# Mixing stage: query head sums in column groups, low-rank products in row halves, v centred by head in its transpose, and no place pads

## The chip, the cores and the metric

The kernel runs on one core of a Trainium2 chip. A core has five engines with a queue each: PE (TensorE; the loading of its weights is listed apart, as PEld), DVE (VectorE), ACT (ScalarE), POOL (GpSimd) and SP (SyncE, which here only issues transfers). Each engine takes its instructions in the order of its queue; engines wait for each other by semaphores. [...] The metric is device microseconds for one execution, the median of the runs shown.

## The reference

Two layers of a decoder trunk on 512 tokens of width 1024, in float32. A layer is a half-step SwiGLU feed-forward, a mixing sub-layer, and another half-step feed-forward, each behind a modulated RMS norm. The change lies in the mixing sub-layer, which has three head groups side by side: attention with a window of 128 and sinks (8 query heads, 2 key heads of 64), RWKV-7 time mixing (4 heads of 64) and a short convolution. What matters of it:

```python
# attention: q and k are normed by head
q = rms_norm(q.reshape(B, T, ATT_Q_HEADS, HEAD_DIM), q_gain)
...
# RWKV: decay and rate come from low-rank products
w_log = -jax.nn.softplus(-(w0 + jnp.tanh(wd) @ w_w2).astype(f32)) - 0.5
a = jax.nn.sigmoid((a0 + ad @ w_a2).astype(f32))
...
def step(S, inp):
    r_t, w_t, k_t, v_t, kk_t, a_t = inp
    s_kk = jnp.einsum('bhvk,bhk->bhv', S, kk_t)
    S = (S * w_t[:, :, None, :] - s_kk[..., None] * (kk_t * a_t)[:, :, None, :]
         + v_t[..., None] * k_t[:, :, None, :])
    return S, jnp.einsum('bhvk,bhk->bhv', S, r_t)
...
mean = jnp.mean(y, axis=-1, keepdims=True)
var = jnp.mean(jnp.square(y - mean), axis=-1, keepdims=True)
y = ((y - mean) * lax.rsqrt(var + RWKV_GN_EPS)).reshape(B, T, RWKV_WIDTH) * gn_w + gn_b
bonus = jnp.sum(r * k * r_k, axis=-1, keepdims=True) * v
```

The recurrence is linear in v, and each row of the state belongs to one element of v. So if v has mean zero over a head, y has too.

## The kernel before

Activations are held transposed: 128 channels on the partitions, 512 tokens along them. Large products are split in two float32r parts of each operand and made of three matmuls (`mm3`, L117 to L123): `ps_mm` products of 512 columns, or of 256 in the feed-forward, where a block scheme with sums of operands (`com`) saves products. Small products of the mixing stage are plain float32: PE makes two passes for one such matmul, and the trace records each pass (a transpose is one).

The mixing sub-layer (`mix`, L583) is written as generators. `products` (L634) makes the input projection in twenty tiles of 128 channels in the order k, v, four tiles of q, then those of RWKV and the convolution, and later the first part of the output projection. `rwkv(q)` (L745) runs for two head pairs, `attention` (L985) for four blocks of 128 tokens. A loop (L1081 to L1094) steps the live generators and, by the figures that these yield and by RWKV_WORK, ATT_WORK and FILL_WORK (L35), deals out product steps between them. The order of each engine's queue then comes from the framework's scheduler, which goes by priorities and its own estimate of times: instructions of one product step can get between those of another generator, and an ordering edge between two instructions, or a block of high priority, changes that.

Where the change touches it:

- **Query head sums** (L670 to L688). Each q tile holds two heads of 64 channels. It is copied to `qr`, squared by ACT (`qsq`), and for each block of 128 tokens the square is the weight (128x128) and `bones2` (two columns, one for each head) the moving operand: `ps_q` gets tokens on the partitions and two sums. ACT takes the root into `rq`, DVE the reciprocal after the fourth tile. `attention` uses `rq` as a scale by token in its softmax (L1015 to L1026); its score tiles (`ps_sc`) and the sums take their PSUM banks from the same two ("x").
- **Low-rank products** (L752 to L756). `lo` holds tanh(wd) in partitions 0 to 63 and ad in 64 to 127, `lw` the two matrices likewise. `ps_w` and `ps_a` are one matmul each, of 64 rows, 128 columns of weights and 512 of moving operand.
- **v turned** (`tmajor`, L850; `tcopy(v_[q], "vN")`, L868). The recurrence needs v with tokens on the partitions: four transposes into `ps_vN`, a copy by ACT.
- **Mean over a head** (L964 to L966). `headsum` (L608) multiplies y by `bones`, the block matrix of ones of a head, into `ps_m`; DVE subtracts the mean. Then follow the square (`gnsq`), its head sum (`ps_v`), the root (`gnrs`), the reciprocal and the scaling, the gate (`ps_g`), and the split of y for the last output products (`yrH`, `yrL`, L1097 to L1110).
- **Places.** `con` holds the constants (L52; the first 128 columns are loaded at the start, L145, the rest at L1214). A pad of GAP = 448 bytes a partition stands ahead of the pools of `hn` (L67), one of 64 behind them (L70), and two of the same sizes around `com` in the feed-forward (L345, L347). So `hn` and `com` lie 448 bytes, modulo 512, off the weights `wH` and `wL`, and `act` and all that is behind lies level with them.

Of the kernel before, what the change touches and what calls it, by code (L numbers as in the profile page):

```python
# [8 lines left out]
F32 = mybir.dt.float32  # L9
F32R = mybir.dt.float32r  # L10
I32 = mybir.dt.int32
AF = mybir.ActivationFunctionType
ALU = mybir.AluOpType
AXL = mybir.AxisListType
ORDER = mybir.DependencyInfo(mybir.DependencyClass.NoSync, mybir.DependencyReason.DATA)
SYNC = mybir.DependencyInfo(mybir.DependencyClass.Sync, mybir.DependencyReason.DATA)

P = 128
D = 1024
T = 512  # L20
# [6 lines left out]
NB = T // P  # L27
CH = 64
# [3 lines left out]
PAD = 24  # L32
GAP = 448
GROUPS = ((0, 12), (12, 22))
RWKV_WORK, ATT_WORK, FILL_WORK = 29.8, 15.2, 129.6  # L35


def _columns(spec):
# [13 lines left out]
CON, NCON = _columns((  # L52
    ("ident", P), ("bones", P), ("bones2", 2), ("su", CH), ("iu", CH), ("diag", CH),
    ("lev0", CH), ("lev1", CH), ("i64", CH), ("mc", P), ("mp", P), ("mq", P),
# [4 lines left out]
def trunk_kernel(ctx, tc, ins, out, layers=L, phases=("ffn1", "mix", "ffn2")):  # L59
    nc = tc.nc  # L60
# [5 lines left out]

    shift = ctx.enter_context(tc.tile_pool(name="shift", bufs=1))  # L67
    shift.tile([P, GAP // 4], F32, name="shift")
    hnp = [ctx.enter_context(tc.tile_pool(name=n, bufs=KD)) for n in ("hnp", "hnp2")]
    shift = ctx.enter_context(tc.tile_pool(name="shift2", bufs=1))  # L70
    shift.tile([P, (512 - GAP) // 4], F32, name="shift2")
    sp = ctx.enter_context(tc.tile_pool(name="sp", bufs=2))
    ps = ctx.enter_context(tc.tile_pool(name="ps", bufs=4, space=PSUM))
    dram = ctx.enter_context(tc.tile_pool(name="dram", bufs=1, space=bass.MemoryType.DRAM))
    tt, stt, ts = nc.vector.tensor_tensor, nc.vector.scalar_tensor_tensor, nc.vector.tensor_scalar
    act, mm = nc.scalar.activation, nc.tensor.matmul
# [7 lines left out]
    def psum(shape, name, tag="x"):  # L84
        return ps.tile(shape, F32, name=name, tag=tag, bufs=2)
# [87 lines left out]
    def cst(name):  # L173
        a, b = CON[name]
        return con[:, a:b]
# [161 lines left out]
    def ffn(l, w_in, w_pair, w_out, hn, im, ss, need, then, first, ready, coming):  # L337
# [6 lines left out]
        with tc.tile_pool(name="act", bufs=1) as ap_:  # L344
            ap_.tile([P, GAP // 4], F32, name="gap", tag="gap")  # L345
            com = {n: tuple(ap_.tile([P, 4, H2], F32R, name=x, tag="com", bufs=8) for x in ("comH", "comL")) for n in ("P1", "P2", "T3", "T4")}
            ap_.tile([P, (512 - GAP) // 4], F32, name="gap2", tag="gap2")  # L347
            n_first = 2 if first is None else 4
# [234 lines left out]
    def mix(l, hn, ss, mp, then, ready):  # L583
# [18 lines left out]
        def EA(name):  # L602
            return mp.tile([P, T], F32, name=name, tag="ea", bufs=3)
# [4 lines left out]
        def headsum(src, name, tag="x"):  # L608
            pt = psum([P, T], name, tag)
            mm(pt, cst("bones"), src, start=True, stop=True)  # L610
            return pt

        chunks = lambda t: t.rearrange("p (c t) -> p c t", t=CH)
        blocks = lambda t: t.rearrange("p (b c) -> p b c", c=P)
# [19 lines left out]
        def products():  # L634
# [33 lines left out]
            rq = small("rq", NB * 8)  # L668
            rq4 = rq.rearrange("p (b i g) -> p b i g", i=4, g=2)
            for i in range(4):  # L670
                pt = yield from tile_()
                copied = nc.scalar.copy(pt.like(qr[:, i]), pt.view)
                if i == 0:
                    latest["act"] = copied
                if i == 1:
                    pk = headsum(ksq, "ps_ks")
                    rk = EA("rk")
                    act(rk, pk, AF.Sqrt, bias=vals["eps"], scale=1.0 / CH)
                    nc.vector.reciprocal(rk, rk)
                    stt(kt, kt, gqk, rk, ALU.mult, ALU.mult)  # L680
                sq = EA("qsq")
                act(pt.like(sq), pt.view, AF.Square)
                yield
                pq = psum([P, NB, 2], "ps_q")
                for b in range(NB):
                    mm(pq[:, b], sq[:, b * P : (b + 1) * P], cst("bones2"), start=True, stop=True)
                act(rq4[:, :, i], pq, AF.Sqrt, bias=vals["eps64"])
            nc.vector.reciprocal(rq, rq)  # L688
            got.update(kt=kt, V=V, qr=qr, rq=rq)
            done.add("att")  # L690

            got["lo"] = shifted((yield from tile_()), 6, S(1, "lo"))
            act(got["lo"][:64], got["lo"][:64], AF.Tanh)
            for q in range(2):
# [50 lines left out]
        def rwkv(q):  # L745
# [6 lines left out]
            pw = psum([P, T], "ps_w", R)  # L752
            mm(pw, lw[:64, cw], lo[:64], start=True, stop=True)
            pa = psum([P, T], "ps_a", R)
            mm(pa, lw[64:, cw], lo[64:], start=True, stop=True)
            yield 1.7  # L756
            kp = prm(l, "kk")[:, c1]
# [92 lines left out]
            def tmajor(src, name):  # L850
                pt = psum([P, NB, P], name, R)
                for b in range(NB):
                    nc.tensor.transpose(pt[:, b], src[:, b * P : (b + 1) * P], cst("ident"))
                return pt
# [108 lines left out]

            pm = headsum(y, "ps_m", R)  # L964
            stt(y, pm, -1.0 / CH, y, ALU.mult, ALU.add)
            yield 0.9  # L966
            sq = EQ(q, "gnsq")
# [322 lines left out]
def lay_out(i):  # L1290
# [58 lines left out]

    con = [r == s, r // CH == s // CH, r // CH == np.arange(2)[None, :], u < v, u <= v]  # L1350
    con += [u // BASE == v // BASE, lower(4, u, v), lower(5, u, v)]
# [19 lines left out]
```

## Time and profile before

| | |
|---|---|
| median of 3 runs | 1866.85 us (1865.7 to 1868.2) |
| the profiled execution | 1866.04 us |
| its span, first to last instruction | 1864.0 us |
| mean granted PE clock | 0.994 |
| mixing sub-layer, layer 0 | about 390 to 615 us |
| mixing sub-layer, layer 1 | about 1304 to 1529 us |

A row of the timeline gives the start, the duration, engine, line and operation, the tile written and those read, and the number of instructions merged in the row; in brackets the idle time ahead of it and what ended it. Matmuls are pipelined, so one that is listed with 0.38 us takes PE for less: the steps between starts tell the price. A row of the grouped view gives busy time and mean nanoseconds of one instruction. A row of waits gives microseconds in total, times, and the longest.

### The profile page before, as it was taken

To read this page: it belongs to the slowest core of one execution; us is meant where nothing else is said; L and a number is where in the kernel's file an instruction comes from. 1 tells how busy PE (TensorE), PEld (TensorE's weight loads), DVE (VectorE), ACT (ScalarE), POOL (GpSimd) and SP (SyncE) were. 2 spreads that over 40 slices of the span, in tenths; PEclk is the share of its full clock that TensorE was granted. 3 is DMA by queue.
4 is the path that set the end of the run, shared out by engine and by line. 5 is a ranking of instruction groups with operands and counts; after the bars stand their busy time and mean duration, and the time that the engine had idled before them with its cause. 6 is when DMAs were issued, how large, how long until landed. Compare 5 with 4: busy or idle time off the path is not lost.

```text
span 1864.0 us, 33421 instructions
## 1 busy us (share of the span) xinstructions
PE 1828.7 (98%) x13664; PEld 1644.4 (88%) x13664; DVE 1398.4 (75%) x2202; ACT 836.3 (45%) x1272; POOL 130.9 (7%) x212
## 2 busy tenths in 40 slices
PE   8999999999999999999999999999999999999999
PEld 6889899986777999899999988999767788998998
DVE  7687677867986887777878786777589778874872
ACT  4443255346422555245345524544563335532551
POOL 0101110100000000110100020110000000100100
PEclk8999999999999999999999999999999999999999
DMA  7667876621122475886737688773212125775752
GB/s 307 225 185 234 263 197 202 221 83 46 58 55 72 136 195 176 296 223 195 246 112 197 171 272 228 192 229 114 101 56 59 53 68 161 209 227 139 203 144 68
DMA packets 104313, 308.24 MB, mean 165 GB/s; under 512 B 23392, under 2 KB 24416, under 8 KB 103136
## 3 DMA queue, kind: packets, MB, share of 16 engines
q1 hardware_dynamic: 75936, 203.34, 32.3%
q0 software_dynamic: 28224, 102.77, 21.7%
q8 instruction: 107, 1.75, 0.4%
q14 instruction: 46, 0.38, 0.1%
HBM read 302.66 MB, written 3.41 MB: 164 GB/s over the span
## 4 chain that ended last, share of the span: by engine, by line
PE 71%; DVE 13%; DMA 7%; issue 4%; ACT 4%; POOL 1%; SPq 0%; POOLq 0%; DVEq 0%; ACTq 0%
PE ps_mm L121 11%; PE ps_mm L122 10%; PE ps_mm L123 10%; PE ps_d L420 6%; PE ps_d L422 6%; PE ps_d L421 6%; PE ps_f L420 3%; PE ps_f L422 3%; PE ps_f L421 3%; DMA wada<-in_wadaT 2%; DVE wL L135 2%; PE ps_g L422 2%; PE ps_g L420 2%; PE ps_g L421 2%; ACT wH L133 1%
## 5 line engine op out<-in xcount | busy, mean ns | idle before, releaser
L133 ACT CAST wH<-wraw 128x1024 fp32r<-128x1024 f32 (+2 forms) x292 | 266.1, 918 | 434.7 <-PE ps_mm L122 190.2
L135 DVE TENSOR_TENSOR wL<-wraw,wH 128x1024 fp32r<-128x1024 f32 (+2 forms) x292 | 307.2, 1058 | 105.1 <-ACT wH L133 104.4
L123 PE MATMUL ps_mm<-actH,wL 128*128 128x512 f32 (+1 forms) x784 | 281.5, 359 | 2.8 <-DVE wL L135 2.8
L121 PE MATMUL ps_mm<-actH,wH 128*128 128x512 f32 (+1 forms) x784 | 281.6, 359 | 0.0
L122 PE MATMUL ps_mm<-actL,wH 128*128 128x512 f32 (+1 forms) x784 | 281.2, 359 | 0.0
L121 PE MATMUL ps_mm<-hnH,wH 128*128 128x512 f32 (+1 forms) x760 | 267.5, 359 | 5.7 <-ACT hnH L133 2.9
L122 PE MATMUL ps_mm<-hnL,wH 128*128 128x512 f32 (+1 forms) x760 | 266.5, 353 | 0.5
L123 PE MATMUL ps_mm<-hnH,wL 128*128 128x512 f32 (+1 forms) x760 | 266.4, 353 | 0.6 <-DVE wL L135 0.6
L420 PE MATMUL ps_d<-comH,wH 128*128 128x256 f32 x816 | 224.7, 275 | 0.3 <-ACT s L446 0.3
L421 PE MATMUL ps_d<-comL,wH 128*128 128x256 f32 x816 | 224.4, 275 | 0.0
L422 PE MATMUL ps_d<-comH,wL 128*128 128x256 f32 x816 | 224.4, 275 | 0.0
L192 DVE SCALAR_TENSOR_TENSOR wada<-wada,crep 128x1024 f32<-128x1024 f32 x140 | 167.7, 1219 | 48.8 <-DMA wada<-in_wadaT 48.2
L135 DVE TENSOR_TENSOR wL<-sum,wH 128x1024 fp32r<-128x1024 f32 x102 | 124.9, 1224 | 71.5 <-ACT wH L133 71.3
L123 PEld LDWEIGHTS ps_mm<-actH,wL 128*128 128x128 f32 x784 | 149.1, 190 | 20.3 <-DVE wL L135 3.6
L121 PEld LDWEIGHTS ps_mm<-hnH,wH 128*128 128x128 f32 x760 | 143.4, 191 | 24.9 <-issue 3.8
L121 PEld LDWEIGHTS ps_mm<-actH,wH 128*128 128x128 f32 x784 | 149.1, 190 | 16.8
L122 PEld LDWEIGHTS ps_mm<-actL,wH 128*128 128x128 f32 x784 | 149.0, 190 | 16.8
L123 PEld LDWEIGHTS ps_mm<-hnH,wL 128*128 128x128 f32 x760 | 145.5, 191 | 19.3 <-issue 4.3
L122 PEld LDWEIGHTS ps_mm<-hnL,wH 128*128 128x128 f32 x760 | 145.4, 192 | 17.2 <-DVE hnL L277 1.6
L420 PEld LDWEIGHTS ps_d<-comH,wH 128*128 128x128 f32 x816 | 156.7, 192 | 0.9 <-ACT s L446 0.9
L422 PEld LDWEIGHTS ps_d<-comH,wL 128*128 128x128 f32 x816 | 156.7, 192 | 0.0
L421 PEld LDWEIGHTS ps_d<-comL,wH 128*128 128x128 f32 x816 | 156.7, 192 | 0.0
(354 smaller groups left out, 3855.6 us busy)
## 6 DMA issues: line engine op xcount, KB each, us to landing
wada<-in_wadaT POOLq DMA_DIRECT2D x128, 512.0 KB, 4.8
wraw<-in_wmi SPq DMA_DIRECT2D x40, 512.0 KB
wraw<-in_w2p SPq DMA_DIRECT2D x36, 512.0 KB
wraw<-in_w1p SPq DMA_DIRECT2D x32, 512.0 KB
wraw<-in_w1o SPq DMA_DIRECT2D x32, 384.0 KB
wraw<-in_w2o SPq DMA_DIRECT2D x32, 384.0 KB
wraw<-in_w1i SPq DMA_DIRECT2D x20, 512.0 KB
wraw<-in_w1o SPq DMA_DIRECT2D x32, 320.0 KB
```

The lines of the kernel that those rows point to most:

```text
L121: mm(acc, wH, xH, start=start, stop=False)
L122: mm(acc, wH, xL, start=False, stop=False)
L123: mm(acc, wL, xH, start=False, stop=stop)
L133: nc.scalar.copy(hi, src)
L135: return nc.vector.tensor_sub(lo, src, hi.bitcast(F32))
L192: stt(w, w, 1.0, crep, ALU.mult, ALU.mult, accum_out=out_)
L420: mm(acc, wH, xH, start=start and i + k == 0, stop=False, skip_group_check=True)
L421: mm(acc, wH, xL, start=False, stop=False, skip_group_check=True)
L422: mm(acc, wL, xH, start=False, stop=k == 3, skip_group_check=True)
```

## The change

Query head sums: the squares of all four q tiles are kept. When the fourth is there, four matmuls take `bones2`, now 32 columns of which two are not zero, as the weight and one square each as the moving operand, and write partitions 0 to 31, 32 to 63, 64 to 95 and 96 to 127 of one PSUM tile; they are put behind each other by ordering edges (`after`) at high priority. One root over the whole tile goes into the place of the first square, four transposes bring tokens to the partitions, and the reciprocal reads them from PSUM.

Low-rank products: each is cut in two halves of 256 columns, and the four matmuls alternate between rows 0 to 63 and 64 to 127, chained the same way; the two head pairs are in one chain. The yield behind them is 1.2 in place of 1.7.

v is turned by a matmul with `cen`, the identity less 1/64 within a head, in place of the transposes, so it comes out centred. The mean of y and its subtraction go, with their yield of 0.9. RWKV_WORK falls from 29.8 to 28.9.

All four place pads go. `con` grows by 158 columns.

```diff
-GAP = 448
-RWKV_WORK, ATT_WORK, FILL_WORK = 29.8, 15.2, 129.6
+RWKV_WORK, ATT_WORK, FILL_WORK = 28.9, 15.2, 129.6
...
-    ("ident", P), ("bones", P), ("bones2", 2), ("su", CH), ("iu", CH), ("diag", CH),
+    ("ident", P), ("bones", P), ("bones2", 32), ("cen", P), ("su", CH), ("iu", CH), ("diag", CH),
...
-    shift = ctx.enter_context(tc.tile_pool(name="shift", bufs=1))
-    shift.tile([P, GAP // 4], F32, name="shift")
     hnp = [ctx.enter_context(tc.tile_pool(name=n, bufs=KD)) for n in ("hnp", "hnp2")]
-    shift = ctx.enter_context(tc.tile_pool(name="shift2", bufs=1))
-    shift.tile([P, (512 - GAP) // 4], F32, name="shift2")
...
-            ap_.tile([P, GAP // 4], F32, name="gap", tag="gap")
             com = {n: tuple(ap_.tile([P, 4, H2], F32R, name=x, tag="com", bufs=8) for x in ("comH", "comL")) for n in ("P1", "P2", "T3", "T4")}
-            ap_.tile([P, (512 - GAP) // 4], F32, name="gap2", tag="gap2")
...
+        def after(m, other):
+            tc.add_manual_dep(m.ins, other.ins.name, ORDER, reason="parts of the array run together")
+            return m
...
+            sqs = []
             for i in range(4):
...
-                sq = EA("qsq")
-                act(pt.like(sq), pt.view, AF.Square)
+                if i % 2 == 0:
+                    sqs += (lambda t: [t[:, 0], t[:, 1]])(U(1, "qsq", [P, 2, T]))
+                behind = act(pt.like(sqs[i]), pt.view, AF.Square)
                 yield
-                pq = psum([P, NB, 2], "ps_q")
-                for b in range(NB):
-                    mm(pq[:, b], sq[:, b * P : (b + 1) * P], cst("bones2"), start=True, stop=True)
-                act(rq4[:, :, i], pq, AF.Sqrt, bias=vals["eps64"])
-            nc.vector.reciprocal(rq, rq)
+            pq = psum([P, T], "ps_q")
+            with tc.high_priority():
+                for i, sq in enumerate(sqs):
+                    behind = after(mm(pq[32 * i : 32 * i + 32], cst("bones2"), sq, start=True, stop=True), behind)
+            root = sqs[0]
+            act(root, pq, AF.Sqrt, bias=vals["eps64"])
+            yield
+            pr = psum([P, NB, 4, 32], "ps_rq")
+            for b in range(NB):
+                nc.tensor.transpose(pr[:, b].rearrange("p i z -> p (i z)"), root[:, b * P : (b + 1) * P], cst("ident"))
+            nc.vector.reciprocal(rq4, pr[:, :, :, :2])
...
-            act(got["lo"][:64], got["lo"][:64], AF.Tanh)
+            got["tanh"] = act(got["lo"][:64], got["lo"][:64], AF.Tanh)
...
-            mm(pw, lw[:64, cw], lo[:64], start=True, stop=True)
             pa = psum([P, T], "ps_a", R)
-            mm(pa, lw[64:, cw], lo[64:], start=True, stop=True)
-            yield 1.7
+            behind = got.get("lora", got["tanh"])
+            with tc.high_priority():
+                for sl in HALVES:
+                    for pt, half in ((pw, slice(0, 64)), (pa, slice(64, P))):
+                        behind = got["lora"] = after(mm(pt[:, sl], lw[half, cw], lo[half, sl], start=sl is HALVES[0], stop=sl is HALVES[1]), behind)
+            yield 1.2
...
-                    nc.tensor.transpose(pt[:, b], src[:, b * P : (b + 1) * P], cst("ident"))
+                    x = src[:, b * P : (b + 1) * P]
+                    if name == "ps_vN":
+                        mm(pt[:, b], x, cst("cen"), start=True, stop=True)
+                    else:
+                        nc.tensor.transpose(pt[:, b], x, cst("ident"))
...
-            pm = headsum(y, "ps_m", R)
-            stt(y, pm, -1.0 / CH, y, ALU.mult, ALU.add)
-            yield 0.9
...
-    con = [r == s, r // CH == s // CH, r // CH == np.arange(2)[None, :], u < v, u <= v]
+    con = [r == s, r // CH == s // CH, r // CH == np.arange(32)[None, :], (r == s) - (r // CH == s // CH) / CH, u < v, u <= v]
```

## The prediction

> **What bounds the kernel now.** I read the busy shares first, then the stages of one mixing sub-layer (layer 0, about 390 to 600 us; layer 1 repeats it 914 us later), then who PE waited for, and last PE's own timeline around each operation that the change touches.
>
> ```profile
> span 1864.0 us, 33421 instructions
> PE 1828.7 (98%) x13664; PEld 1644.4 (88%) x13664; DVE 1398.4 (75%) x2202; ACT 836.3 (45%) x1272; POOL 130.9 (7%) x212
> ```
>
> The stages follow; the columns are length, then busy time of PE, PEld, DVE, ACT and POOL, with counts.
>
> ```profile
> 390.00:430.00 40.00, 38.62 (x200) 30.69 (x198) 21.43 (x37) 23.79 (x49) 0.00 (x0) 1.00 0.28 93
> 430.00:470.00 40.00, 38.45 (x207) 25.66 (x206) 34.17 (x80) 23.36 (x60) 0.42 (x2) 1.00 0.17 56
> 470.00:510.00 40.00, 39.45 (x226) 29.51 (x225) 35.78 (x94) 20.04 (x44) 0.43 (x2) 1.00 0.21 63
> 510.00:550.00 40.00, 39.61 (x704) 31.01 (x703) 31.35 (x74) 9.10 (x16) 0.00 (x0) 1.00 0.25 62
> ```
>
> PE is full in every stage, because the projection matmuls fill whatever attention and RWKV leave. From 430 to 510, though, DVE is busy 70 us of 80 and nearly as short as PE. The longest waits of PE between 388 and 560 us are these:
>
> ```profile
> PE ps_pt L1041 <- DVE Sc L1029: 1.8, 3, 1.0
> PE ps_c L811 <- DVE B L814: 0.6, 2, 0.4
> ```
>
> The other five lines are 0.3 or less each, and the whole list comes to 3.7 us. So a microsecond taken out of PE's stream is a microsecond off the end, unless it is taken where DVE is about to become the one that is waited for. Off the mixing stage the program is the same, apart from addresses. I therefore sum PE time. Two prices are needed throughout, and both stand around the mean over a head in layer 1; the rows of DVE and ACT behind it are used later.
>
> ```profile
> 1503.58 0.38 PE L123 MATMUL ps_mm<-y2H,wL 128*128 128x512 f32 x1
> 1503.79 1.02 PE L610 MATMUL ps_m<-y,con 128*128 128x512 f32 x2
> ...
> 1504.87 0.38 PE L122 MATMUL ps_mm<-y3L,wH 128*128 128x512 f32 x1
> ```
>
> ```profile
> 1504.85 0.69 DVE L965 SCALAR_TENSOR_TENSOR y<-ps_m,y 128x512 f32<-128x512 f32 x1 [3.02 <-PE ps_m L610]
> ...
> 1506.06 0.62 ACT L968 ACTIVATE gnsq<-y 128x512 f32<-128x512 f32 x1
> ```
>
> A projection matmul of 512 columns holds PE for one step, 1503.79 - 1503.58, 0.215 more closely (its row says 0.38, which is its way through the array). A float32 product of 512 columns, two passes, costs 1504.87 - 1503.58 less two such steps: 0.86.
>
> **The query head sums.** Now each of the four q tiles has its own sum: four blocks of sq as 128x128 weights with 2 moving columns, recorded as two passes each.
>
> ```profile
> L686 PE MATMUL ps_q<-con,qsq x64: 251/251/272, 392.9 to 1327.7; 128*128 128x2 f32 x64
> ```
>
> That is 8 records a tile, 8 tiles in two layers. Their price is read from the starts around them, first tile and last tile of layer 0:
>
> ```profile
> 392.67 0.38 PE L121 MATMUL ps_mm<-hnH,wH 128*128 128x512 f32 x1
> 392.94 1.05 PE L686 MATMUL ps_q<-con,qsq 128*128 128x2 f32 x8
> ...
> 394.16 0.38 PE L123 MATMUL ps_mm<-hnH,wL 128*128 128x512 f32 x1
> ...
> 412.73 0.38 PE L123 MATMUL ps_mm<-hnH,wL 128*128 128x512 f32 x1
> 413.07 1.05 PE L686 MATMUL ps_q<-con,qsq 128*128 128x2 f32 x8
> 414.05 1.14 PE L1003 MATMUL ps_sc<-kt,qr 64*128 64x128 f32 x8
> ```
>
> Between 392.67 and 394.16 (1.49 us) lie two projection matmuls, so the sum costs 1.06. The last: 414.05 - 412.73 - 0.215 = 1.10. Four are 4.3 us a layer. These include the short wait for the squaring on ACT, four times.
>
> After: bones2 (32 columns) is the weight and sq moves, 512 columns in fp32, each product into its own 32 output partitions: 4 x 2 records. The trace has no group of 32 columns, but one of 64 (attention times V, two groups) and one full-height product:
>
> ```profile
> 446.22 1.08 PE L1059 MATMUL ps_av<-pmc,V 128*64 128x512 f32 x4
> 447.13 1.03 PE L1059 MATMUL ps_av<-pmp,V 128*64 128x512 f32 x4
> 448.09 0.70 PE L610 MATMUL ps_kk<-kksq,con 128*128 128x512 f32 x1
> ```
>
> Eight records of 512 columns take 448.09 - 446.22 = 1.87 us, 0.23 each, where one by one they would take 0.43 each (half of 0.86): two column groups run at once. Four at once would be 0.93, and with some 0.2 for going in and out and for the last wait 1.2. The bounds: 1.2 (four at once), 2.1 (two), 3.7 (one by one). I take 1.2, since the groups of the row share nothing that four would not. Four transposes turn the root back; like ps_vt and ps_vN they are single passes, 0.5 (worked out for ps_vN below). After is 1.7 against 4.3: **2.6 us a layer saved**, with 1.7 and 0.1 as the other ends.
>
> [...]
>
> ACT exchanges four small roots for one of 128x512, about 0.7 us by the 0.62 of the squaring row above, hidden under product steps; the reciprocal stays one of 32 elements a partition:
>
> ```profile
> 414.46 0.35 DVE L688 RECIPROCAL rq<-rq 128x32 f32<-128x32 f32 x1 [1.17 <-ACT rq L687]
> ```
>
> In PE's queue the transposes wait for the root, which itself can stand behind a weight cast on ACT, and all projection work queued behind them waits too; one product step is put between. If that cover is short, PE stands up to 1 us a layer; I take 0. The scores' second bank now waits for the reciprocal (two banks, sums and turned root take both). Three sums no longer stand ahead of the last q tile, so it is squared 3.2 us earlier; sums, root, transposes, reciprocal and an estimated 0.5 for the hand-overs (1.2 + 0.7 + 0.5 + 0.4 + 0.5) bring the scores to about 413.1 against 414.05, so attention is not late.
>
> **The low-rank products.** ps_w (rows 0 to 63) and ps_a (rows 64 to 127) stand apart now:
>
> ```profile
> 442.57 0.38 PE L123 MATMUL ps_mm<-hnH,wL 128*128 128x512 f32 x1
> 442.88 1.12 PE L753 MATMUL ps_w<-lo,lw 64*128 64x512 f32 x2
> 443.93 0.66 PE L1041 MATMUL ps_pt<-con,Sc 128*128 128x128 f32 x4
> ...
> 444.86 0.38 PE L123 MATMUL ps_mm<-hnH,wL 128*128 128x512 f32 x1
> 445.17 1.12 PE L755 MATMUL ps_a<-lo,lw 64*128 64x512 f32 x2
> ```
>
> Each costs 1.36 - 0.215 = 1.15 (443.93 - 442.57; 446.22 - 444.86), 2.3 for both. After, the two alternate in pieces of 256 columns, 8 records. The scores have that very shape:
>
> ```profile
> 429.82 0.38 PE L123 MATMUL ps_mm<-hnH,wL 128*128 128x512 f32 x1
> 430.13 1.13 PE L1001 MATMUL ps_sc<-kt,qr 64*128 64x256 f32 x8
> ...
> 431.51 0.38 PE L122 MATMUL ps_mm<-hnL,wH 128*128 128x512 f32 x1
> ```
>
> 1.69 - 0.43 = 1.26. Saved 1.0 a head pair, **2.1 us a layer**. If other work gets between them, 0 (and 0.2 worse for twice the records). But they lie in the stretch where DVE is 70 of 80 busy: PE comes to the next DVE-bound step earlier and may just wait there, so I count half, 1.0.
>
> **The centring.** v is multiplied by a centring matrix in place of the transposes, two passes for one:
>
> ```profile
> 474.85 0.66 PE L853 MATMUL ps_vN<-con,v 128*128 128x128 f32 x4
> ...
> 475.56 0.38 PE L122 MATMUL ps_mm<-hnL,wH 128*128 128x512 f32 x1
> ...
> 368.93 0.28 PE L123 MATMUL ps_mm<-actH,wL 128*128 128x256 f32 x1
> 369.04 0.61 PE L268 MATMUL ps_rstd<-con,rstd 128*128 128x128 f32 x4
> ...
> 369.60 0.28 PE L122 MATMUL ps_mm<-actL,wH 128*128 128x256 f32 x1
> ```
>
> The four transposes: 475.56 - 474.85 - 0.215 = 0.50. Four fp32 records of 128 columns: 369.60 - 368.93 less two steps of 0.11 = 0.45, eight 0.9; the 8 narrow records above (1.06) are the other end. **It adds 0.4 to 0.56 a pair, 0.9 a layer.** In return the mean over the head (ps_m) goes, 0.86 a pair, **1.7 us a layer saved**, and its subtraction, 0.69 us of DVE (the row of L965). In the second pair's tail the squaring also comes some 2 us earlier, which keeps the chain to the last products ahead of PE's shortened stream; in itself it is worth nothing more, as PE is the one that is full.
>
> **The pads, the larger constants, the work figure.** With the pads (448 and 64 bytes) gone, hn and com lie level with the weights, as act does already; and everything behind the constants moves by 632 bytes or what that is rounded to. The two placements can be compared:
>
> ```profile
> L421 PE MATMUL ps_d<-comL,wH 128*128 128x256 f32 x816 | 224.4, 275 | 0.0
> ...
> L122 PE MATMUL ps_mm<-actL,wH 128*128 128x256 f32 x160 | 44.0, 275 | 0.0
> ```
>
> Shifted (com) and level (act) both show 275 ns: I count 0. The 632 bytes a partition are 81 kB more in one early load, under 0.5 us at the 165 GB/s of the span, and no wait follows; 0.3. The work figure changes only how product steps are dealt out among RWKV's steps; 0, with 1 us either way.
>
> **The sum.** Full: 2.6 + 2.1 + 1.7 - 0.9 = 5.5 a layer, 11 in all. With half of the low-rank gain (-2.1) and the load (-0.3), 8.6. The profiled execution took 1866.04 us, 2.0 beyond its span, and lies 0.8 under the median of 1866.85. 1866.04 - 8.6 = 1857.4; at the median about **1858 us**.
>
> **Rivals.**
> (a) *DVE's chain sets the pace from 414 to 510.* For it: 70 of 80 us. Against: PE's waits there are only part of 3.7 us. Then the low-rank gain and half the query gain vanish: 3.4 + 2.6 - 1.8 = 4.2, 1862.6.
> (b) *The column groups run one by one*, each load waiting for the matmul before it, or other work getting between them. Against it: ps_av. Then 5.0 of the 8.6 is lost (2.5 a layer): 1863.2. [...]
> (c) *The places cost.* One mechanism: moving and weight operands at equal places get in each other's way. For it: the warm-up matmuls, whose two operands are one tile:
>
> ```profile
> 6.47 5.94 PE L1196 MATMUL ps_warm<-ones_r 128*128 128x512 f32 x25
> ```
>
> (5.94 - 0.38) / 24 = 0.232 us a step against 0.215. About 1,560 products of hn with 512 columns and 6,400 of hn or com with 256 move level after the change. At 17 ns and half of it, 27 + 54 = 81 us: 1866.85 - 8.6 + 81 = 1939. From about 1.1 ns each (8.6 us over 8,000) it outweighs the gain. Against: act, level already, is as fast.
> (d) *No change that can be told*: gains are eaten by a reshuffled order of PE's queue, up to 1 us of standing for the root a layer and waits on ps_c and ps_pt; about 1865.
>
> **How the numbers follow.** The forecast has 0.62, (a) 0.13, (b) 0.07, (c) 0.10, (d) 0.08. A difference of 0.2% (3.7 us) is about what a measurement of this kernel can tell from none. Faster by more takes the forecast and most of (a) and (b), which end at that line (1863.1): 0.78; the same 0.10 ((d) and the upper edge of (a) and (b)); slower 0.12 ((c), and (d) gone worse). Low end: all 11 and the four waits for the squaring beyond it, some 3.5 more: 1852. High end: past (b) and (d), where (c) at an eighth of its price would also lie: 1868.
>
> **What would show it.** Right: ps_q shows 8 records a layer, starting four at a time, within 1.2 us; ps_w and ps_a in pairs within 1.3; no ps_m; vN's eight records in about 0.9; the step of hn and com products still 0.215 and 0.11; PE's waits still under 5 us a layer. Wrong: ps_q records 0.43 apart; PE idle at the turned root or at ps_c; a longer step; or the FFN stages changing length.

## The result, and the profile after

The median is 1880.05 us over 15 runs (1868.97 to 1885.44) against 1866.85 for the kernel before, also over 15: a ratio of **1.0056, interval 1.0042 to 1.0070**. The change makes the kernel 0.56% slower, where 0.5% faster was forecast. The page of the profiled execution of after (1881.69 us):

```profile
span 1879.6 us, 33373 instructions
PE 1831.1 (97%) x13648; PEld 1645.1 (88%) x13648; DVE 1395.5 (74%) x2198; ACT 835.3 (44%) x1266; POOL 131.2 (7%) x212
```

Where the time is: the step of the projection matmuls is unchanged (0.215 us), and the mixing sub-layer, which I measure from the copy of kt to the last product of yrH with wH, is longer. These are its two ends in layer 0, before and after:

```profile
390.18 0.59 ACT L655 COPY kt<-ps_mm 128x512 f32<-128x512 f32 x1 [1.97 <-PE ps_mm L123]
...
614.73 0.28 PE L121 MATMUL ps_mm<-yrH,wH 128*128 128x256 f32 x1
```

```profile
387.36 0.58 ACT L653 COPY kt<-ps_mm 128x512 f32<-128x512 f32 x1 [1.97 <-PE ps_mm L118]
...
618.09 0.28 PE L116 MATMUL ps_mm<-yrH,wH 128*128 128x256 f32 x1
```

224.5 us became 230.7, and layer 1 shows 224.3 and 230.6: 12.5 of the 15.6 us between the two profiled executions. The other 3 stand outside: 2.8 us less ahead of the first mixing, 2.9 and 3.2 more behind the two. There each trace has some 20 us at half clock (a granted clock of 0.5), in other places, so the clock does not explain the sum of these; what does stays open.

The stages of after, the same four as the prediction showed of before, in the columns of that view (the number behind the five engines is the granted PE clock):

```profile
387.00:427.00 40.00, 36.29 (x174) 27.87 (x174) 21.13 (x37) 22.81 (x44) 0.00 (x0) 0.98 0.33 106
427.00:467.00 40.00, 36.57 (x185) 24.89 (x185) 29.56 (x71) 23.14 (x60) 0.43 (x2) 0.97 0.09 31
467.00:507.00 40.00, 40.00 (x241) 29.01 (x238) 33.80 (x95) 18.89 (x43) 0.00 (x0) 0.88 0.17 49
507.00:547.00 40.00, 38.08 (x624) 30.14 (x622) 31.60 (x75) 9.72 (x17) 0.43 (x2) 1.00 0.28 73
```

Two columns changed. PE is busy 36.3 and 36.6 us in the first two stages, where it was 38.6 and 38.5. And the clock, 1.00 in all four before, is 0.98, 0.97 and 0.88: 40 us x (0.02 + 0.03 + 0.12) = 6.8 us of clock are missing. Narrower windows say where: two of before, then the same two of after, and the matching ones of its layer 1.

```profile
420.00:430.00 10.00, 8.63 (x40) 5.80 (x38) 6.41 (x14) 8.99 (x26) 0.00 (x0) 1.00 0.01 2
460.00:480.00 20.00, 19.23 (x159) 11.84 (x158) 18.09 (x43) 10.84 (x32) 0.42 (x2) 1.00 0.23 54
```

```profile
420.00:430.00 10.00, 7.48 (x35) 4.32 (x35) 5.94 (x13) 6.64 (x19) 0.00 (x0) 0.83 0.18 63
460.00:480.00 20.00, 17.23 (x108) 10.63 (x107) 17.10 (x41) 7.84 (x25) 0.43 (x2) 0.74 0.15 41
...
1340.00:1350.00 10.00, 7.48 (x32) 5.44 (x31) 6.31 (x14) 8.35 (x25) 0.00 (x0) 0.84 0.17 54
1385.00:1400.00 15.00, 12.02 (x82) 6.89 (x82) 14.12 (x35) 5.63 (x21) 0.42 (x2) 0.77 0.07 17
```

The trace's clock events read 0.5 for 3.4 us from 425.3 and for 10.2 us from 466.2 (0.17 x 10 / 0.5 = 3.4; 0.26 x 20 / 0.5 = 10.4), and in layer 1 for 6.8 us from 1346.9 and 6.8 from 1391.3: 13.6 us at half clock a layer, 6.8 lost. Before has none in either mixing.

Ahead of each stretch PE had stood still. PE's longest waits in the mixing of after (total, times, longest), 385 to 560 us:

```profile
PE ps_pt L1051 <- DVE Sc L1039: 3.0, 3, 2.1
PE ps_bo L603 <- DVE bonus L797: 1.6, 2, 1.3
PE ps_c L820 <- DVE a L806: 1.4, 1, 1.4
PE ps_q L687 <- ACT qsq L682: 1.2, 1, 1.2
PE ps_s L967 <- ACT y L962: 1.0, 1, 1.0
```

With two lines of 0.5 and 0.2 they come to 8.9 us, against 3.7 before. In PE's timeline of after they stand here:

```profile
406.03 0.38 PE L118 MATMUL ps_mm<-hnH,wL 128*128 128x512 f32 x1
406.34 1.06 PE L687 MATMUL ps_q<-qsq,con 128*32 128x512 f32 x6
408.57 1.04 PE L687 MATMUL ps_q<-qsq,con 128*32 128x512 f32 x2 [1.18 <-ACT qsq L682]
409.55 0.48 PE L116 MATMUL ps_mm<-hnH,wH 128*128 128x512 f32 x1
...
410.30 0.38 PE L116 MATMUL ps_mm<-hnH,wH 128*128 128x512 f32 x1
410.52 0.60 PE L693 MATMUL ps_rq<-con,qsq 128*128 128x128 f32 x4
...
422.23 0.63 PE L1051 MATMUL ps_pt<-con,Sc 128*128 128x128 f32 x4 [0.40 <-DVE Sc L1039]
424.98 0.82 PE L1051 MATMUL ps_pt<-con,Sc 128*128 128x128 f32 x4 [2.12 <-DVE Sc L1039]
...
463.23 1.12 PE L603 MATMUL ps_bo<-bonus,con 128*128 128x512 f32 x2 [1.35 <-DVE bonus L797]
465.78 2.65 PE L820 MATMUL ps_c<-AR,a 64*64 64x128 f32 x32 [1.42 <-DVE a L806]
```

The 2.12 us end at 424.98, and half clock begins at 425.3; the 1.35 and 1.42 end at 465.78, and it begins at 466.2. The same 32 products of ps_c show 2.65 us where they showed 1.76 before. Before, the second pair's low-rank products stood around ps_bo and were its cover:

```profile
461.76 1.12 PE L753 MATMUL ps_w<-lo,lw 64*128 64x512 f32 x2
462.82 1.13 PE L610 MATMUL ps_bo<-bonus,con 128*128 128x512 f32 x2
463.87 1.12 PE L755 MATMUL ps_a<-lo,lw 64*128 64x512 f32 x2
465.09 1.76 PE L811 MATMUL ps_c<-AR,a 64*64 64x128 f32 x32
```

After the change all 16 records of both pairs run from 428.5 to 430.5, because the two pairs are in one chain at high priority.

So the balance of one mixing is: all gaps in PE's stream sum to 4.4 us before and 9.4 after; 6.8 us go to the half clock. What is left is work: 224.5 - 4.4 = 220.1 before, 230.7 - 9.4 - 6.8 = 214.5 after. **The work fell by 5.6 us a layer, near the full sum of 5.5; 5.0 of it became waits, and 6.8 us of clock were lost on top.**

The 15 runs bear this out. With the mean of (1 - clock) x span as time lost to the clock, after loses 18.1 us a run and 35 runs of before lose 9.1; the means of what is left of the times are 1860.1 and 1859.5. (The 35 runs were taken beside e1 to e4.) So a mean run loses 9.0 us more to the clock than before, and not the 2 x 6.8 of the profiled execution, which is one of the three with the lowest clock (0.987).

### The profile page after: what moved, and what is told of

Its sections match the earlier page's. It is cut to its first block, busy times and chain, and to the rows that moved or that the text cites. A ratio compares the mean times of both kernels' runs of the same rounds, so it can differ in the third digit from the quotient of the medians.

```text
span 1879.6 us, 33373 instructions
## 1 busy us (share of the span) xinstructions
PE 1831.1 (97%) x13648; PEld 1645.1 (88%) x13648; DVE 1395.5 (74%) x2198; ACT 835.3 (44%) x1266; POOL 131.2 (7%) x212
## 4 chain that ended last, share of the span: by engine, by line
PE 66%; DVE 15%; DMA 10%; issue 4%; ACT 4%; POOL 1%; SPq 0%; POOLq 0%; ACTq 0%; DVEq 0%
PE ps_mm L116 9%; PE ps_mm L117 9%; PE ps_mm L118 8%; PE ps_d L413 6%; PE ps_d L414 6%; PE ps_d L415 6%; PE ps_f L415 3%; PE ps_f L413 3%; PE ps_f L414 3%; DMA wada<-in_wadaT 3%; DVE wL L130 3%; DVE wada L187 2%; ACT wH L128 2%; PE ps_g L415 2%; PE ps_g L413 2%
## 5 line engine op out<-in xcount | busy, mean ns | idle before, releaser
L414 PE MATMUL ps_d<-comL,wH 128*128 128x256 f32 x816 | 225.0, 276 | 0.0
L117 PEld LDWEIGHTS ps_mm<-actL,wH 128*128 128x128 f32 x784 | 149.1, 190 | 16.8
```

The source lines that it names most:

```text
L117: mm(acc, wH, xL, start=False, stop=False)
L414: mm(acc, wH, xL, start=False, stop=False, skip_group_check=True)
```

## The experiments

The texts on record use these letters. A: PE lost its cover, stands still, and the clock halves. B: the new places cost. C: centring costs more than it saves. D: the half clock comes by itself or from something else, and only work and waits count. P: PE's stream sets the length. Q: the chain through DVE and ACT is as long, so that work taken out of PE turns into waits. In the table "clock" is the mean time lost to the clock, beside that of before on the same chip; the last two columns are of the profiled execution, layer 0 and layer 1.

| run | ratio to before, interval | clock, us | mixing, us | half clock in it, us |
|---|---|---|---|---|
| before | 1 | 9.1 | 224.5, 224.3 | 0, 0 |
| after | 1.0056, 1.0042 to 1.0070 | 18.1 | 230.7, 230.6 | 13.6, 13.6 |
| e1_places | 1.0000, 0.9983 to 1.0016 | 9.8 (9.1) | 224.4, 224.4 | 0, 0 |
| e2_q_back | 1.0002, 0.9987 to 1.0017 | 15.1 (9.1) | 225.7, 226.5 | 6.8, 10.2 |
| e3_lora_back | 1.0010, 0.9995 to 1.0025 | 11.8 (9.1) | 226.8, 225.4 | 3.4, 0 |
| e4_cen_only | 0.9993, 0.9976 to 1.0011 | 9.6 (9.1) | 225.0, 225.7 | 0, 0 |
| e5_busy | 1.0027, 1.0015 to 1.0039 | 9.2 (9.2) | 226.6, 226.5 | 0, 0 |
| e6_lora_late | 1.0012, 1.0000 to 1.0025 | 10.7 (9.2) | 226.5, 226.2 | 3.4, 3.4 |
| e8_both | 1.0018, 1.0008 to 1.0027 | 11.6 (9.2) | 225.6, 225.4 | 0, 0 |
| e9_late_busy | 1.0039, 1.0025 to 1.0052 | 11.2 (9.2) | 225.4, 225.6 | 0, 0 |
| e10_less_fill | 1.0026, 1.0013 to 1.0040 | 16.8 (8.6) | 227.4, 225.9 | 10.2, 6.8 |
| e11_dve_short | 0.9988, 0.9978 to 0.9998 | 12.6 (8.6) | 221.6, 221.9 | 3.4, 3.4 |
| e12_before_dve_short | 1.0041, 1.0026 to 1.0055 | 9.9 (8.6) | 227.9, 227.1 | 0, 0 |
| e13_real_cover | 1.0036, 1.0016 to 1.0056 | 12.3 (9.4) | 228.4, 228.9 | 6.8, 6.8 |

### The parts of the change

e1: the kernel before without its pads and with the larger constants.

```diff
-    shift.tile([P, GAP // 4], F32, name="shift")
...
-            ap_.tile([P, GAP // 4], F32, name="gap", tag="gap")
...
-    ("ident", P), ("bones", P), ("bones2", 2), ("su", CH), ("iu", CH), ("diag", CH),
+    ("ident", P), ("bones", P), ("bones2", 32), ("cen", P), ("su", CH), ("iu", CH), ("diag", CH),
...
```

> The kernel before with only the places of the change: no pads, constants 158 columns larger; the instructions are those of before. Theory A (PE lost its cover: work was taken from PE where attention and RWKV wait for DVE and ACT, PE stands idle there, and the granted clock is halved behind the idle): as before, ratio 0.998 to 1.002, no half clock between 390 and 615 us. Rival B (the places cost): 1.004 or more, spread over all stages.

No difference: the places cost less than can be told (the interval ends at 0.16%, 3 us), and theory B falls.

e2: after with the four sums of before, one behind each q tile.

```diff
-                    behind = after(mm(pq[32 * i : 32 * i + 32], cst("bones2"), sq, start=True, stop=True), behind)
...
+                    mm(pq[:, b], sq[:, b * P : (b + 1) * P], cst("bones2")[:, :2], start=True, stop=True)
```

> The changed kernel with the query head sums of before. Theory A: the idle of PE at the fourth sum (1.2 us) and the 2.1 us ahead of the second turned block shrink to what before had (1.05), the half clock near 425 goes; idle ahead of ps_bo and ps_c and the half clock near 466 stay. About 3 us a layer less than the change: ratio 1.001 to 1.004. Rival B: as the change, 1.005 to 1.007.

e3: after with the low-rank products of before, uncut and without priority.

```diff
...
-                        behind = got["lora"] = after(mm(pt[:, sl], lw[half, cw], lo[half, sl], start=sl is HALVES[0], stop=sl is HALVES[1]), behind)
-            yield 1.2
...
+            mm(pw, lw[:64, cw], lo[:64], start=True, stop=True)
...
+            mm(pa, lw[64:, cw], lo[64:], start=True, stop=True)
+            yield 1.7
```

> The changed kernel with the low-rank products of before, apart and with the yield of 1.7. Theory A: the second pair's products stand again where ps_bo and ps_c wait for DVE, the idle there (1.35 and 1.42 us) and the half clock near 466 go; what goes wrong at 407 to 429 stays. About 4 us a layer less than the change: ratio 0.999 to 1.003. Rival B: as the change, 1.005 to 1.007.

Each undoes one pair of place and stretch. e2 has no half clock near 425, but near 463, behind waits of 0.49 and 1.42 us at ps_bo and ps_c, and near 1381. In e3 PE no longer waits at ps_bo and waits 0.09 us at the first ps_c, with no half clock near 466, but the 2.13 us before the second ps_pt stand, with 3.4 us of half clock in layer 0 and none in layer 1, for the same wait. With either part taken back, no difference from before can be told; together they make the loss. e2's ratio lies under the 1.001 to 1.004 of theory A, and the clock hides a gain there: less the time lost to it, the runs of e2 are 4.1 us shorter than those of before (1855.4 against 1859.5), and it took 6.0 more (15.1 against 9.1).

e4: only the centring and the places, here against before.

```diff
-                    nc.tensor.transpose(pt[:, b], src[:, b * P : (b + 1) * P], cst("ident"))
+                    x = src[:, b * P : (b + 1) * P]
+                    if name == "ps_vN":
+                        mm(pt[:, b], x, cst("cen"), start=True, stop=True)
...
-            pm = headsum(y, "ps_m", R)
-            stt(y, pm, -1.0 / CH, y, ALU.mult, ALU.add)
```

> The changed kernel with the query head sums and the low-rank products of before: only the centring and the places are left. Theory A: PE work falls by 0.8 us a layer where PE is full, no new idle between 405 and 470: 1863 to 1867, ratio 0.998 to 1.000. Rival B: 1.004 or more. Rival C (the centring itself, two passes in place of one, is what costs): 1.001 to 1.003.

Theory C's 1.001 to 1.003 lies at the end of the interval or beyond it. The 0.8 us a layer that this part saves on PE (1.7 - 0.9) would be 0.1%, too little for these runs to tell; in the profiled execution it isn't seen: mixing is 0.5 and 1.4 longer, with a new wait of 1.1 us before ps_o.

### Does standing still halve the clock?

e5: useless work in the places where PE stood still in after, some 10 us in all.

```diff
+                if b == 0 and turns[0] == 1:
+                    busy(pt.rearrange("p i q -> p (i q)"), 9, turns[1])
...
+                for x in (kk, k2):
+                    mm(pb, cst("bones"), x, start=True, stop=True)
...
+                    busy(pts[0].rearrange("p b a t -> p (b a t)"), 6, summed)
```

> The changed kernel with TensorE kept busy where it idles: nine one-pass products of a matrix of ones before the second ps_pt of the first block, two more head sums (of kk and k2) before the ps_bo of the first pair, six products of ones before its first ps_c. Some 5 us of useless work a layer (9 x 0.22, 2 x 0.86, 6 x 0.22) stand in about 4.9 us of idle time. Theory A (the idle time makes the chip halve the clock, and the halved clock is the loss): no stretch at half clock in the mixing, its length falls from 230.7 to 224 to 227 us, ratio to before 0.997 to 1.002 in place of 1.0056. Rival D (the stretches at half clock come by themselves or from something else, and what counts is how much work and waiting there is): half clock near 425 and 466 us as before, mixing 230 to 236, ratio 1.005 to 1.010.

The windows of after's stretches, in e5:

```profile
420.00:430.00 10.00, 9.57 (x49) 6.05 (x47) 5.95 (x13) 8.08 (x22) 0.00 (x0) 1.00 0.26 71
460.00:480.00 20.00, 18.51 (x138) 11.62 (x137) 17.55 (x38) 10.27 (x29) 0.43 (x2) 1.00 0.23 50
...
1340.00:1350.00 10.00, 9.56 (x45) 6.82 (x45) 6.48 (x14) 8.82 (x25) 0.00 (x0) 1.00 0.19 55
1385.00:1400.00 15.00, 14.60 (x124) 9.68 (x123) 14.01 (x29) 6.31 (x18) 0.00 (x0) 1.00 0.20 54
```

0.83, 0.74, 0.84 and 0.77 became 1.00, and over 12 runs the time lost to the clock is 9.2 us, that of before. With 10 us of work more the kernel is faster than after: the intervals against before do not overlap. So theory A holds for the clock, and D falls. The ratio is a little over the range given: less the time lost to the clock, the runs are 4.3 us longer than those of after (1864.4 against 1860.1), as added work that does not fall on idle time is still time.

e10 puts the same question to the kernel before, with none of the change in it.

```diff
...
-        mm(acc, wL, xH, start=False, stop=stop)
+        if not less:
+            mm(acc, wL, xH, start=False, stop=stop)
```

> The kernel before with less work for TensorE where it only fills: of three of the last product tiles of the mixing (14 to 16) the third of three terms is left out, 24 matmuls of 0.216 us, 5.2 us a layer. It asks whether a microsecond out of TensorE's stream is a microsecond off the end, as the prediction took it. Theory P (TensorE's stream sets the length): mixing 219 to 220 in place of 224.4 us, ratio 0.994 to 0.996. Theory Q (a chain through VectorE and ScalarE is as long as the stream, so that work taken out turns into waits): mixing 223 to 225, TensorE's idle time in it 8 to 9 us in place of 4.4, ratio 0.999 to 1.001, or up to 1.004 where the clock halves for it.

24 product matmuls a layer are gone, 10.4 us in all, and the kernel is slower by 0.26%. The wait, and the clock behind it:

```profile
502.08 0.38 PE L122 MATMUL ps_mm<-hnL,wH 128*128 128x512 f32 x1
504.94 1.12 PE L611 MATMUL ps_bo<-bonus,con 128*128 128x512 f32 x2 [2.48 <-DVE bonus L789]
506.88 1.56 PE L812 MATMUL ps_c<-AR,a 64*64 64x128 f32 x16 [0.82 <-DVE a L798]
```

```profile
500.00:520.00 20.00, 15.85 (x185) 12.07 (x184) 18.11 (x31) 2.92 (x3) 0.42 (x2) 0.74 0.36 88
...
1420.00:1440.00 20.00, 15.85 (x191) 12.12 (x190) 19.58 (x31) 2.62 (x3) 0.43 (x2) 0.83 0.36 95
```

PE reached ps_bo of the second pair earlier, stood 2.48 us, and the clock halved. That is the mechanism of after, made by taking work away. It speaks against P; Q named the direction, though its mixing is longer than Q's 223 to 225. PE's gaps in the mixing grew from 4.4 to 8.3 us, so 3.9 of the 5.2 us a layer became waits. Less the time lost to the clock, the runs are 3.5 us shorter than those of before (1855.1 against 1858.6), so here too the loss is the clock's (16.8 against 8.6 us).

### Can the savings be had?

e6: after without priority for the low-rank products, so that the second pair's cover ps_bo again.

```diff
-            with tc.high_priority():
+            if True:
                 for sl in HALVES:
```

> The changed kernel without the priority of the low-rank products, so that those of the second pair stand around ps_bo again; the products of the two row halves are then mostly apart in the queue. Theory A: the waits of ps_bo and ps_c fall from 1.35 and 1.42 to under 0.5 us, no half clock near 466; the wait of 2.1 us before the second ps_pt stays, and with it half clock near 425 at times; mixing 225 to 229, ratio 0.999 to 1.003. Rival D: half clock near 466 as in the changed kernel, mixing 229 to 231, ratio 1.004 to 1.007.

e8: e6, and three product steps ahead of the sums.

```diff
+            for _ in range(3):
+                assert next(tiles) is None
+            behind = lastpe[0]
             with tc.high_priority():
```

> As the one before, and three product steps are given out and ordered ahead of the sums of the four column groups. Theory A: the wait of the fourth sum falls from 1.2 to about 0.5 us, but the products are taken from those behind, so that the wait before the second ps_pt is as long or longer (2.1 to 2.8 us) and half clock stands near 425 in both layers; mixing 225 to 229, ratio 0.999 to 1.003. Rival (the uncovered wait of the fourth sum is what matters): mixing 223 to 225, ratio 0.995 to 0.999.

e9: e8, and nine products of ones before the second ps_pt.

```diff
+                if b == 0 and turns[0] == 1:
+                    busy(pt.rearrange("p i q -> p (i q)"), 9, turns[1])
```

> As the one before, and nine products of ones (1.9 us) before the second ps_pt of the first block. Theory A: no stretch at half clock in the mixing; its length 222 to 225 us, so that part of what the change saves is seen: ratio 0.995 to 1.000. Rival (VectorE's chain sets the pace, the savings of TensorE are hidden): no half clock, but 224 to 226, ratio 0.999 to 1.002. Rival D: half clock stays, mixing 228 to 232, ratio 1.003 to 1.008.

e6 went as theory A has it: ps_bo and ps_c wait 0.07 and 0.36 us, half clock is left only at the 2.13 us of ps_pt. e8 has the shorter wait at ps_q (0.49) and the full wait at ps_pt (2.13), but no half clock in the mixing of its profiled execution, so such a wait does not always bring it. e9's profiled execution (1869.53 us) has no half clock in the mixing, but it was the fastest of six; the ratio lies where rival D put it, without D's half clock or its length of the mixing, and why the other runs are longer stays open (over the six runs 2.0 us of the difference are clock and 4.2 are not).

e11 and e12 leave out two reciprocals of the first pair, 5.7 us of DVE a layer, in after and in before.

```diff
-            nc.vector.reciprocal(iP, Pt)
-            nc.vector.reciprocal(rn, rn)
+            if q:
+                nc.vector.reciprocal(iP, Pt)
+                nc.vector.reciprocal(rn, rn)
+            else:
+                ts(iP, Pt, 0.0, 1.0, ALU.mult, ALU.add)
+                ts(rn, rn, 0.0, 0.1, ALU.mult, ALU.add)
```

> The changed kernel with a shorter chain on VectorE: the two reciprocals of the first pair (iP and rn, 3.35 us each) are replaced by writes of a constant of about 0.5 us, 5.7 us a layer less (these two results are left out). Theory Q (the waits of ps_bo and ps_c are VectorE's chain coming late): these waits fall from 1.35 and 1.42 to under 0.5 us, no half clock near 466, mixing 221 to 225, ratio 0.996 to 1.001; the half clock near 425 may stay. Theory P (what counts is TensorE's order and stream): waits move elsewhere, mixing 226 to 230, ratio 1.001 to 1.005.

> The same cut of VectorE's chain in the kernel before (the two reciprocals of the first pair are left out). Theory P: TensorE was busy 220.6 of 225 us, its stream sets the length, so mixing 223 to 225, ratio 0.998 to 1.001. Theory Q: the chain set it as much, so mixing 220 to 222, ratio 0.996 to 0.998 (no more than TensorE's 4.4 us of idle time can go).

In after it went as Q has it: the wait at ps_bo is 0.44 us, none stands at ps_c, no half clock near 466, and the mixing is 9 us shorter. In before the same cut made the kernel slower, against both theories. PE's longest waits there:

```profile
PE ps_pt L1045 <- DVE Sc L1033: 1.8, 3, 1.0
PE ps_o L946 <- DVE N L937: 1.7, 1, 1.7
PE ps_x L901 <- DVE T L892: 1.5, 1, 1.5
PE ps_mm L122 <- DVE y4L L135: 1.0, 1, 1.0
```

ps_o and ps_x, later in the chain, now wait in their turn; that the products which covered them were spent earlier is my reading and was not tried. The clock is near that of before (9.9 against 8.6 us), so this loss is waits: PE's gaps sum to 9.3 us against 4.4.

e13: real work in place of e9's useless work. The second ps_pt is ordered behind a later product, and only the first pair's low-rank products keep priority.

```diff
+    GATES = {90: 'pt2'}
...
-            with tc.high_priority():
+            with tc.high_priority() if q == 0 else nullcontext():
```

> The changed kernel with work of its own in the place of the longest idle time, nothing added: the second ps_pt of the first block is ordered behind a later product (so that six product matmuls and the low-rank products of the first pair, 2.25 us, stand ahead of it), and only the first pair's low-rank products keep their priority (half of the second pair's then stands between ps_bo and ps_c). Theory A (idle time that halves the clock, and savings that became waits): the wait of 2.1 us before that ps_pt falls under 0.3, no half clock near 425, that near 466 gone or shorter; mixing 220 to 223 us, ratio 0.995 to 0.999, under the kernel before. Rival (the savings are taken back by VectorE's chain wherever the work stands): waits come up elsewhere, mixing 224 to 226, ratio 0.999 to 1.003.

Slower than before, beyond both ranges. PE's timeline there, then DVE's:

```profile
421.84 0.63 PE L1062 MATMUL ps_pt<-con,Sc 128*128 128x128 f32 x4 [0.40 <-DVE Sc L1050]
424.98 0.76 PE L116 MATMUL ps_mm<-hnH,wH 128*128 128x512 f32 x1 [2.52 <-DVE lo L635]
```

```profile
423.30 0.18 DVE L1049 RECIPROCAL den<-den 128x4 f32<-128x4 f32 x1
423.39 0.46 DVE L635 SCALAR_TENSOR_TENSOR lo<-ps_mm,par,lo 128x256 f32<-128x256 f32 x1
423.76 0.68 DVE L1050 TENSOR_TENSOR Sc<-Sc,den 128x512 f32<-128x512 f32 x1
424.36 0.47 DVE L635 SCALAR_TENSOR_TENSOR lo<-ps_mm,par,lo 128x255 f32<-128x255 f32 x1
```

The product that was to cover the wait waits itself: it needs the PSUM tile that `lo` is copied out of, and that copy stands in DVE's queue among the same softmax steps as Sc. In after, too, the copy ran at 423.78 to 425.2, at the end of PE's 2.12 us. So in this order of the products none was ready that PE could have done there; another order was not tried. The products came only as far ahead as their tiles were emptied (2.52 us of waiting here), so time saved on PE ahead of that point became waiting. No version that computes the whole came out faster than before: e4's 0.9993 can't be told from 1.

## Why the prediction was wrong

**The step that failed** is the one from PE's time to the end: "So a microsecond taken out of PE's stream is a microsecond off the end, unless it is taken where DVE is about to become the one that is waited for." The prediction charged its own exception with 1.0 us a layer, half of the low-rank gain, and put all other waits in its sum at 0. Of the 5.6 us a layer that came out, 5.0 turned into waits (in e10, without the change, 3.9 of 5.2), and the waits cost more than they hold, because the granted clock fell (another 6.8 us a layer in the profiled execution). The clock stood in the rows that the prediction quoted, 1.00 in each stage of the mixing, and the prediction took it as given. None of the rivals has it. (a), DVE's pace, and (d), gains eaten by waits on ps_c and ps_pt, had the half of the mechanism that ends at 1862.6 or about 1865; less the time lost to the clock, after and before are the same within 0.6 us.

**The cover of the query sums.** Of the turned root the prediction wrote "If that cover is short, PE stands up to 1 us a layer; I take 0", and this 0 held: four product matmuls ran between the sums and ps_rq (409.55 to 410.52), with no gap. The gap came one step earlier, in "some 0.2 for going in and out and for the last wait": the fourth sum waited 1.18 us for its square (0.83 in layer 1). ACT made that square at 407.92, behind a weight cast and the copy of q, and between the last product of the fourth tile and its sum PE's queue held nothing but the other three sums. The yield in the products' own generator deals out no product step there.

**The low-rank products.** The prediction asked whether other work gets between them, and not what their leaving uncovers. Their old place was the cover of ps_bo and ps_c, and the move takes that away: waits of 1.35 and 1.42 us in layer 0, and 5.1 us of clock behind them, against the 1.0 that was charged (e6 gives the cover back).

**The prices were right in sum.** The column groups do run together: 6 records of 512 columns in 1.06 us, three groups at once, and not one by one as rival (b) had it. All six weight loads of these records were done 0.15 us after the first began (406.33), with the first matmuls in flight on the same rows. From 406.34 to 409.55 less the wait, the sums took 2.0 us, not 1.2, with the fourth alone; with 0.5 for the transposes that saves 1.8 us a layer, not 2.6. Centring and low-rank, from PE's timeline of after:

```profile
428.49 0.57 PE L764 MATMUL ps_w<-lo,lw 64*128 64x256 f32 x1
...
430.50 1.07 PE L1069 MATMUL ps_av<-pmc,V 128*64 128x512 f32 x2
...
478.99 1.16 PE L864 MATMUL ps_vN<-con,v 128*128 128x128 f32 x8
479.90 0.46 PE L116 MATMUL ps_mm<-hnH,wH 128*128 128x512 f32 x1
```

16 low-rank records take 2.0 us for both pairs (2.5 predicted, 4.6 before), the eight of vN 0.91 (0.9 predicted). That the full sum of 5.5 us a layer met a measured 5.6 is in part luck, as the query sums saved 0.8 less and the low-rank products 0.5 more than their terms. Rival (c), the places, is refuted by e1.

**Its own signs** were well chosen: of "PE idle at the turned root or at ps_c" the second half came true, and "PE's waits still under 5 us a layer" is what the trace of after contradicts first (8.9).

## What to carry to other kernels

Where an engine is full only because filler work covers its waits, a saving on it can be worth nothing (5.0 of 5.6 us a layer became waits), so name first what stands in the place of the work that goes, and whether that filler can run there: here it needed its output buffer emptied by the very engine that was waited for (2.52 us in e13). When matmul work is moved or cut, look for gaps in PE's stream of 1 us and more, and at the granted clock beside each, for a gap can cost more than its length (behind the 2.12 us of after in layer 0 lay 3.4 us at half clock, 1.7 us lost). A test that adds useless work there tells the clock's share from the rest (e5: 9.2 us a run lost to the clock, against 18.1 in after).

## What the runs showed of the hardware

The granted clock fell to half in stretches of 3.4, 6.8 and 10.2 us. In the mixing they start between 1.0 us before and 1.8 us after the end of a gap in PE's stream. In the profiled executions, single gaps of 2.1 us came with one in 7 of 10 cases (after, e3, e6, e8 and e11, two layers each), gaps of 2.5 us in 4 of 4 (e10, e13); 1.35 and 1.42 us with 1.1 us of work between did in both layers of after, and 0.49 and 1.42 us in both of e2. In the mixing of before, e5 and e9 gaps of 1.24 us and less never did, and in e12 single gaps of 1.52 and 1.66 us did not either. In the feed-forwards smaller ones did: gaps of about 0.6 and 1.05 us with 0.5 us of work between, of which the second stands between 1582 and 1596 us in all 14 traces, came with 3.4 us of half clock in three (after, e1, e5). So gaps of 2.1 us, and in the feed-forwards smaller ones, were followed by half clock in some cases and not in others; what tells these apart was not shown.
